# A decoder layer on one core: in each attention head the 896-column scan is ordered behind the third low part of the weights

## The chip, the cores and the metric

The kernel runs on one of the eight cores of a Trainium2 chip. A core has a matrix engine (TensorE, PE in the profile, its weight loads PEld), a vector engine (VectorE, DVE), a scalar engine for activations (ScalarE, ACT), a general engine (GpSimd, POOL) and a queue that issues transfers (SyncE, SP). Each engine takes its own instructions strictly in the order in which the built program lists them, and waits on semaphores for what others make. The metric is the device time of one execution in microseconds (us), as the median of several.

## The reference

One decoder layer over 1024 positions of width 1024, in float32: token mixing (stick-breaking attention, a state-space mixer, gates), cross-attention into 256 memory tokens, and a feed-forward block. The change lies in the stick-breaking attention, 16 heads of width 64:

```python
def stick_breaking_attention(q, k, v):
    ...
    for blk in range(seq // SB_BLOCK):          # 8 blocks of 128 queries
        t0 = blk * SB_BLOCK
        t1 = t0 + SB_BLOCK
        z = jnp.einsum('bhtd,bhsd->bhts', qf[:, :, t0:t1], kf[:, :, :t1])
        causal = jnp.arange(t1)[None, :] < (t0 + jnp.arange(SB_BLOCK))[:, None]
        log_1mb = jnp.where(causal, jax.nn.log_sigmoid(-z), 0.0)
        tail = lax.cumsum(log_1mb, axis=3, reverse=True)
        w = jnp.where(causal, jnp.exp(z + tail), 0.0)
        outs.append(jnp.einsum('bhts,bhsd->bhtd', w, vf[:, :, :t1]))
```

The weight of a key is its own sigmoid times the product of (1 - sigmoid) over all later keys. Written as differences of running products, that is one scan from the last key to the first.

## The kernel before

The layer is worked off in stages; the one that matters here is the attention stage (lines 770 to 1000 or so), from about 663 to 1086 us of the profiled execution. It handles the 16 heads one after the other, each in two halves of 512 queries, and each half in four blocks of 128 queries. Block b (0 to 7) sees L = (b + 1) x 128 keys.

`scores(h, half, tb, ...)` (lines 896 to 912) makes one block: products of queries and keys into PSUM (tile `sc`, lines 908 and 909), ACT's sigmoid of the negated scores into an SBUF tile `n` of L columns (line 910), and then one VectorE instruction over the L columns, from the last to the first (line 911): it multiplies the running value by the column's `n` and takes the maximum with a mask, so that it leaves running products with ones where the mask forbids the key. This text calls it the scan and names it by its width: 896 columns is block 6. Each tile name has one pool of four buffers for the first half of a head (`n` of up to 512 columns) and one for the second.

`values(h, half, ...)` (lines 915 to 952) turns the running products into outputs, in steps i over tiles of 128 keys. Step i transposes the key tile of the half's blocks on TensorE (tile `tr`, two PSUM buffers, line 925), and splits the result, minus one, into a high part on ACT (`wth`, line 928) and a low part on VectorE (`wtl`, line 929). Three steps later two products with the values, one with each part, add up in PSUM (`av`, lines 937 and 938). In the first half steps i = 0 to 3 make tiles of 512, 384, 256 and 128 columns, so the third low part (i = 2) is the one of 256 columns. In the second half there are four tiles of 512 and then 384, 256 and 128.

Beside these run the projections of the next pair of heads (`mm`, with weights split into `whi` and `wlo`, lines 115 to 132; queries, keys and their low parts `gt`, lines 849 to 870) and, once per pair of heads, a load of value differences and a subtraction on POOL (`va`, line 888) with their split (`v`, lines 115 and 122).

The order on each engine is not the order in which the functions are called. The calls are interleaved by shares (`interleave`), and a list scheduler then places every instruction by its own estimate of times. It pulls the scans of a head's second half ahead, so that they stand among the low parts of the half before. An instruction recorded under `behind([x])` may not be placed ahead of x. On one engine that adds no semaphore; it only fixes who goes first.

Of the kernel before, what the change touches and what calls it, by code (L numbers as in the profile page):

```python
# [8 lines left out]
F32 = mybir.dt.float32  # L9
# [3 lines left out]
ALU = mybir.AluOpType  # L13
# [3 lines left out]
P = 128  # L17
S = 1024
# [36 lines left out]
def hybrid_block(ctx, tc, a, out, dbg=None):  # L55
    nc = tc.nc
    V, A, T = [InTurn(tc, e) for e in (nc.vector, nc.scalar, nc.tensor)]
# [12 lines left out]
    def mk(pl, shape, dt, tag, bufs=None):  # L70
        uid[0] += 1
        kw = {} if bufs is None else {"bufs": bufs}
        return pl.tile(shape, dt, tag=tag, name=f"{tag}_{uid[0]}", **kw)
# [143 lines left out]
    def behind(marks):  # L217

        st = ExitStack()
        for m in marks:  # L220
            st.enter_context(tc.issue_after(m.ins))
        return st
# [52 lines left out]
    with ExitStack() as pa:  # L275
# [24 lines left out]
        with ExitStack() as p1:  # L300
# [135 lines left out]
            pt = mk(psp, [P, HALF], F32, "pdt", bufs=1)  # L436
# [4 lines left out]
            pt = mk(psp, [P, HALF], F32, "pv")  # L441
# [344 lines left out]
        with ExitStack() as p2:  # L786
# [13 lines left out]
            mask = mk(cb_, [P, S], BF16, "mask")  # L800
            V.memset(mask, 0.0)
            G.affine_select(mask[:, S - P:], mask[:, S - P:], [[-1, P]], ALU.is_gt, 1.0, base=0, channel_multiplier=1)

            marks, sig = [], []
            PIN = 8
            FQ = 1

# [73 lines left out]
            def differences(h):  # L881

                j = h % 2
                if j == 0:
                    va, vb = [mk(vp, [P, NCH, P], F32, n, bufs=1) for n in ("va", "vb")]
                    for t, r in ((va, 0), (vb, 1)):
                        nc.sync.dma_start(t, v_d[r:S + r, h * HD:(h + 2) * HD].rearrange("(c p) d -> p c d", p=P))
                    G.tensor_tensor(va, va, vb, ALU.subtract)
                    dvs[0] = va
                dv = dvs[0][:, :, j * HD:(j + 1) * HD]  # L890
                vt = mk(vp, [P, NCH, P], F32R, "v")
                hi_sb(vt[:, :, 0:HD], dv, "p")
                lo_of(vt[:, :, HD:P], dv, vt[:, :, 0:HD], G)
                heads[h]["v"] = vt

            def scores(h, half, tb, ns_):
                def run():
                    hd = heads[h]
                    if half == 0 and tb == 0:
                        differences(h)  # L900
                    b = half * 4 + tb
                    L = (b + 1) * P
                    nt = mk(bp, [P, (half + 1) * HALF], F32, f"n{half}")
                    ns_.append(nt)
                    for s0 in range(0, L, HALF):
                        s1 = min(L, s0 + HALF)
                        ps = mk(psc, [P, HALF], F32, "sc")[:, :s1 - s0]
                        T.matmul(ps, hd["qs"][:, b * P:(b + 1) * P], hd["kh"][:, s0:s1], start=True, stop=False)
                        marks.append(T.matmul(ps, hd["qs"][:, b * P:(b + 1) * P], hd["kl"][:, s0:s1], start=False, stop=True))
                        sig.append(A.activation(nt[:, s0:s1], ps, AF.Sigmoid, scale=-(HD ** -0.5)))  # L910
                    V.tensor_tensor_scan(nt[:, 0:L][:, ::-1], nt[:, 0:L][:, ::-1], mask[:, S - L:][:, ::-1], 1.0, ALU.mult, ALU.max)  # L911
                return run

            LAG = 3
# [1 line left out]
            def values(h, half, ns_):  # L916

                st = {}
                ni = 4 * (half + 1)

                def tr(i):
                    t0 = max(0, i - 4 * half)
                    pt = mk(pst, [P, HALF], F32, "tr")
                    for tb in range(t0, 4):
                        T.transpose(pt[:, tb * P:(tb + 1) * P], ns_[tb][:, i * P:(i + 1) * P], ident)  # L925
                    wh = mk(wt, [P, HALF], F32R, "wth")
                    wl = mk(wt, [P, HALF], F32R, "wtl")
                    A.activation(wh[:, t0 * P:], pt[:, t0 * P:], AF.Identity, bias=mone)  # L928
                    V.scalar_tensor_tensor(wl[:, t0 * P:], pt[:, t0 * P:], -1.0, wh[:, t0 * P:].bitcast(F32), ALU.add, ALU.subtract)  # L929
                    st[i] = (wh, wl, t0 * P)  # L930

                def av(i):
                    if i == 0:
                        st["po"] = mk(psv, [P, HALF], F32, "av")
                    po, vt = st["po"], heads[h]["v"]
                    wh, wl, off = st[i]
                    T.matmul(po[:, off:], vt[:, i, :], wh[:, off:], start=i == 0, stop=False)
                    marks.append(T.matmul(po[:, off:], vt[:, i, :], wl[:, off:], start=False, stop=i == ni - 1))  # L938
                    if i == ni - 1:
                        o = mk(t2, [P, HALF], F32, "oT")  # L940
                        A.activation(o, po, AF.Copy)
                        for j in range(2):
                            nc.sync.dma_start(o_d[j][h * HD:(h + 1) * HD, half * HALF:(half + 1) * HALF], o[j * HD:(j + 1) * HD])

                def step(i):
                    def run():
                        if i < ni:
                            tr(i)
                        if i >= LAG:
                            av(i - LAG)  # L950
                    return run

                return [step(i) for i in range(ni + LAG)]
# [25 lines left out]
            for m in range(NM):  # L979
                h, half = m // 2, m % 2  # L980
# [22 lines left out]
    with ExitStack() as p3:  # L1003
# [36 lines left out]
        marks = []  # L1040
# [409 lines left out]
    marks = []  # L1450
# [815 lines left out]
```

## Time and profile before

| | |
|---|---|
| median of 3 runs | 2505.12 us (2502.95 to 2508.58) |
| profiled execution | 2511.1 us |
| its span, first to last instruction | 2509.4 us |
| mean granted TensorE clock | 0.995 |
| PE busy (share of the span) | 2447.4 us (98%) |
| DVE busy | 1806.5 us (72%) |
| scans (L911), 128 of them | 190.0 us of DVE |
| low parts (L929), 192 of them | 99.7 us of DVE |

A row of the time order reads: start and length in us, engine, line, operation, out<-in by the program's names, partitions x elements, count (x2: two instructions in a row, shown as one), and in brackets the idle time of the engine just before it with what ended it. A row of the waits reads: who waited, for whom, us in total, times, the longest. A row of the stretches reads: the stretch, its length, and for PE, PEld, DVE, ACT and POOL the busy time with the number of instructions, then the granted clock, the DMA share and GB/s. Successive matmuls overlap: the length of one is longer than the distance to the next.

### The profile page before, as it was taken

How to read it: one execution, taken by the hardware profiler on the slowest of the kernel's cores; microseconds unless marked ns; L12 is line 12 of the kernel's file. 1: busy time of each engine (PE TensorE's matmuls, PEld its weight loads, DVE VectorE, ACT ScalarE, POOL GpSimd, SP SyncE). 2: the span in 40 equal slices, each digit the busy share in tenths (PEclk: the TensorE clock that was granted, in tenths of full speed). 3: DMA queues.
4: the chain of work that ended last, by engine and by line, in shares of the span. 5: the costliest groups of instructions: out<-in, count | busy, mean ns of one | idle time of the engine just before them, and what ended most of it. 6: DMA issues, size and time to landing. Idle time of an engine off the chain costs nothing. (4 is left out here: it accounts for less than half of the span.)

```text
span 2509.4 us, 33330 instructions
## 1 busy us (share of the span) xinstructions
PE 2447.4 (98%) x12306; PEld 2015.2 (80%) x12306; DVE 1806.5 (72%) x2237; ACT 1165.5 (46%) x2058; POOL 657.3 (26%) x545
## 2 busy tenths in 40 slices
PE   7999999999999999989999999999999999999998
PEld 5788888888778888877877778888888888888887
DVE  7665877776587888689898774487468655666997
ACT  5333455555465666466644312344435333344433
POOL 3221545443211111134444141102012332220001
PEclk9999999999999999999999999999999999999999
DMA  7431443333534343366332481331241322334322
GB/s 249 157 118 47 141 139 113 104 106 93 156 101 110 89 122 89 89 191 207 108 110 77 129 275 59 120 116 51 84 151 63 103 79 76 95 97 164 131 101 101
DMA packets 249132, 295.62 MB, mean 118 GB/s; under 512 B 17023, under 2 KB 169096, under 8 KB 248842
## 3 DMA queue, kind: packets, MB, share of 16 engines
q1 hardware_dynamic: 248682, 292.45, 37.0%
q8 instruction: 97, 1.59, 0.3%
q10 hardware_dynamic: 288, 1.05, 0.1%
q14 instruction: 65, 0.53, 0.1%
HBM read 202.20 MB, written 74.45 MB: 110 GB/s over the span
## 5 line engine op out<-in xcount | busy, mean ns | idle before, releaser
L911 DVE TENSOR_TENSOR_SCAN n<-n,mask 128x128 f32<-128x128 f32 (+7 forms) x128 | 190.0, 1511 | 24.5 <-ACT n L910 21.2
L122 DVE TENSOR_TENSOR sw<-sf,sw 128x512 fp32r<-128x512 f32 x142 | 126.9, 897 | 72.0 <-ACT sw L119 69.9
L119 ACT ACTIVATE sw<-sf 128x512 fp32r<-128x512 f32 x142 | 88.9, 628 | 155.8 <-PE mm L230 139.1
L928 ACT ACTIVATE wth<-tr,mone 128x512 fp32r<-128x512 f32 x192 | 110.7, 585 | 83.3 <-PE tr L925 81.3
L929 DVE SCALAR_TENSOR_TENSOR wtl<-tr,wth 128x512 fp32r<-128x512 f32 x192 | 99.7, 544 | 48.3 <-ACT wth L928 48.3
L693 DVE SCALAR_TENSOR_TENSOR b<-b,prmT,b 128x1023 f32<-128x1023 f32 (+2 forms) x72 | 109.6, 1522 | 16.9 <-ACT b L687 16.3
L122 DVE TENSOR_TENSOR sw<-wr,sw 128x512 fp32r<-128x512 f32 x107 | 99.2, 929 | 23.9 <-ACT sw L119 23.8
L196 POOL TENSOR_TENSOR sf<-wr,wr 128x512 f32<-128x512 f32 x36 | 53.2, 1477 | 229.8 <-DMA wr<-in_w_gu_dram 82.3
L229 PE MATMUL mm<-h,sw 128*128 128x512 f32 x288 | 112.0, 389 | 0.0
L230 PE MATMUL mm<-h,sw 128*128 128x512 f32 x288 | 111.7, 389 | 0.0
L910 ACT ACTIVATE n<-sc 128x512 f32<-128x512 f32 (+1 forms) x192 | 88.6, 494 | 46.6 <-PE tr L925 28.7
L228 PE MATMUL mm<-h,sw 128*128 128x512 f32 x288 | 109.9, 389 | 0.0
L125 PE MATMUL mm<-oth,bw 128*128 128x512 f32 x256 | 104.5, 408 | 3.9 <-DVE a L1259 2.3
L173 POOL TENSOR_SCALAR rstd<-ms 128x1 f32<-128x1 f32 x74 | 26.9, 363 | 307.8 <-ACT x L180 228.3
L127 PE MATMUL mm<-oth,bw 128*128 128x512 f32 x256 | 101.3, 396 | 0.0
L126 PE MATMUL mm<-otl,bw 128*128 128x512 f32 x256 | 101.1, 395 | 0.0
L127 PE MATMUL p<-bw,h 128*128 128x512 f32 x256 | 100.1, 392 | 0.5 <-DVE h L122 0.5
L126 PE MATMUL p<-bw,h 128*128 128x512 f32 x256 | 99.9, 390 | 0.0
L125 PE MATMUL p<-bw,h 128*128 128x512 f32 x256 | 99.7, 390 | 0.0
L925 PE MATMUL tr<-ident,n 128*128 128x128 f32 x576 | 95.4, 274 | 4.0 <-DVE wtl L929 4.0
L115 POOL TENSOR_SCALAR v<-va 128x512 fp32r<-128x512 f32 x16 | 20.6, 1289 | 286.8 <-PE av L938 165.9
L119 ACT ACTIVATE zh<-zr 128x512 fp32r<-128x512 f32 x72 | 45.0, 631 | 104.7 <-PE ma L492 52.3
(664 smaller groups left out, 7753.9 us busy)
## 6 DMA issues: line engine op xcount, KB each, us to landing
wr<-in_w_in_dram SPq DMA_DIRECT2D x36, 512.0 KB
wr<-in_w_gu_dram SPq DMA_DIRECT2D x72, 256.0 KB
zr<-in_w_in_dram SPq DMA_DIRECT2D x28, 512.0 KB
wraw<-in_w_in_dram SPq DMA_DIRECT2D x20, 512.0 KB
gu_d<-t SPq DMA_DIRECT2D x36, 256.0 KB
zs_d<-zo SPq DMA_DIRECT2D x32, 256.0 KB
xs_d<-b SPq DMA_DIRECT2D x32, 256.0 KB
kl<-gt SPq DMA_DIRECT2D x64, 128.0 KB
```

The lines of the kernel that those rows point to most:

```text
L119: A.activation(o, i, AF.Copy)
L122: eng.tensor_tensor(o, i, hi.bitcast(F32), ALU.subtract)
L125: first = T.matmul(ps, sh, mh, start=start, stop=False)
L126: T.matmul(ps, sh, ml, start=False, stop=False)
L127: T.matmul(ps, sl, mh, start=False, stop=stop)
L228: T.matmul(ps, w[0][:, k, :], bh, start=first and k == 0, stop=False, skip_group_check=True)
L229: T.matmul(ps, w[0][:, k, :], bl, start=False, stop=False, skip_group_check=True)
L230: ins = T.matmul(ps, w[1][:, k, :], bh, start=False, stop=last and k == 3, skip_group_check=True)
L693: V.scalar_tensor_tensor(acc[:, sh:], y[:, :S - sh], cw(3 - sh, f), acc[:, sh:], ALU.mult, ALU.add)
L911: V.tensor_tensor_scan(nt[:, 0:L][:, ::-1], nt[:, 0:L][:, ::-1], mask[:, S - L:][:, ::-1], 1.0, ALU.mult, ALU.max)
L928: A.activation(wh[:, t0 * P:], pt[:, t0 * P:], AF.Identity, bias=mone)
L929: V.scalar_tensor_tensor(wl[:, t0 * P:], pt[:, t0 * P:], -1.0, wh[:, t0 * P:].bitcast(F32), ALU.add, ALU.subtract)
```

## The change

The low parts are noted under head, half and step as they are made. The 896-column scan of a head (block 6, in its second half) is recorded behind the third low part of the same head's first half. The other seven scans of a head and everything else are recorded as before.

```diff
-            marks, sig = [], []
+            marks, sig, lows = [], [], {}
...
-                    V.tensor_tensor_scan(nt[:, 0:L][:, ::-1], nt[:, 0:L][:, ::-1], mask[:, S - L:][:, ::-1], 1.0, ALU.mult, ALU.max)
+                    with behind([lows[h, 0, 2]] if b == 6 else []):
+                        V.tensor_tensor_scan(nt[:, 0:L][:, ::-1], nt[:, 0:L][:, ::-1], mask[:, S - L:][:, ::-1], 1.0, ALU.mult, ALU.max)
...
-                    V.scalar_tensor_tensor(wl[:, t0 * P:], pt[:, t0 * P:], -1.0, wh[:, t0 * P:].bitcast(F32), ALU.add, ALU.subtract)
+                    lows[h, half, i] = V.scalar_tensor_tensor(wl[:, t0 * P:], pt[:, t0 * P:], -1.0, wh[:, t0 * P:].bitcast(F32), ALU.add, ALU.subtract)
```

What the scheduler makes of it shows in the order of the built programs. There a scan is listed as SCALAR_TENSOR_TENSOR with `mask` as its second input, the numbers in the names tell one tile from another, and lines behind 911 are one higher in the new kernel.

VectorE in head 3, around the end of head 2, before. The 896 scan (n_1137) stands between the 768 scan and the last two low parts of head 2 (wtl_6272, wtl_6286):

```order
L911 SCALAR_TENSOR_TENSOR n_1131_6358<-n_1131_6358,mask_5276 128x768
L911 SCALAR_TENSOR_TENSOR n_1137_6378<-n_1137_6378,mask_5276 128x896
L929 SCALAR_TENSOR_TENSOR wtl_6272<-tr_6268,wth_6271 128x256
L929 SCALAR_TENSOR_TENSOR wtl_6286<-tr_6283,wth_6285 128x128
L911 SCALAR_TENSOR_TENSOR n_1144_6403<-n_1144_6403,mask_5276 128x1024
L911 SCALAR_TENSOR_TENSOR n_1158_6465<-n_1158_6465,mask_5276 128x128
```

The same engine in head 3 now, from the key split of the next pair on. wtl_6334, 6355, 6375 and 6394 are the four low parts of head 3's first half, wtl_6448 the first of its second half:

```order
L863 TENSOR_TENSOR gt_6432<-mm_6324,kh_6304 128x512
L912 SCALAR_TENSOR_TENSOR n_1167_6493<-n_1167_6493,mask_5276 128x256
L912 SCALAR_TENSOR_TENSOR n_1176_6528<-n_1176_6528,mask_5276 128x384
L930 SCALAR_TENSOR_TENSOR wtl_6375<-tr_6371,wth_6374 128x256
L912 SCALAR_TENSOR_TENSOR n_1137_6378<-n_1137_6378,mask_5276 128x896
L930 SCALAR_TENSOR_TENSOR wtl_6394<-tr_6391,wth_6393 128x128
L912 SCALAR_TENSOR_TENSOR n_1184_6559<-n_1184_6559,mask_5276 128x512
L930 SCALAR_TENSOR_TENSOR wtl_6448<-tr_6442,wth_6447 128x512
```

The 896 scan went from ahead of head 2's last low parts to between the third and the fourth low part of head 3; the 256 scan of the next head (n_1167) moved down behind the key split too, where it had stood ahead of wtl_6355.

VectorE in head 4, in the same place as the piece above, before (the queries' split, then wtl_6651 and wtl_6670 as third and fourth low part, wtl_6726 the first of the second half):

```order
L854 TENSOR_TENSOR gt_6702<-mm_6600,qs_6586 128x512
L911 SCALAR_TENSOR_TENSOR n_1237_6763<-n_1237_6763,mask_5276 128x256
L911 SCALAR_TENSOR_TENSOR n_1246_6795<-n_1246_6795,mask_5276 128x384
L929 SCALAR_TENSOR_TENSOR wtl_6651<-tr_6647,wth_6650 128x256
L929 SCALAR_TENSOR_TENSOR wtl_6670<-tr_6667,wth_6669 128x128
L911 SCALAR_TENSOR_TENSOR n_1254_6826<-n_1254_6826,mask_5276 128x512
L929 SCALAR_TENSOR_TENSOR wtl_6726<-tr_6720,wth_6725 128x512
```

and now, with the head's 896 scan (n_1209), which had stood eleven rows further up:

```order
L854 TENSOR_TENSOR gt_6702<-mm_6600,qs_6586 128x512
L912 SCALAR_TENSOR_TENSOR n_1237_6763<-n_1237_6763,mask_5276 128x256
L912 SCALAR_TENSOR_TENSOR n_1246_6795<-n_1246_6795,mask_5276 128x384
L930 SCALAR_TENSOR_TENSOR wtl_6651<-tr_6647,wth_6650 128x256
L912 SCALAR_TENSOR_TENSOR n_1209_6657<-n_1209_6657,mask_5276 128x896
L930 SCALAR_TENSOR_TENSOR wtl_6670<-tr_6667,wth_6669 128x128
L912 SCALAR_TENSOR_TENSOR n_1254_6826<-n_1254_6826,mask_5276 128x512
L930 SCALAR_TENSOR_TENSOR wtl_6726<-tr_6720,wth_6725 128x512
```

All else in this piece kept its place: the scan was put in, and what stands behind it moved back by one.

TensorE in head 3, at the first step of its second half (tr_6442 takes the scanned tiles of blocks 4 to 7, of which n_1137 is block 6; av_6397 with wtl_6394 is the product of the first half's fourth low part; mm_6480 is a projection), before:

```order
L925 MATMUL tr_6442<-ident_88,n_1125_6337 128x128
L925 MATMUL tr_6442<-ident_88,n_1131_6358 128x128
L925 MATMUL tr_6442<-ident_88,n_1137_6378 128x128
L925 MATMUL tr_6442<-ident_88,n_1144_6403 128x128
L125 MATMUL mm_6480<-b11h_115,whi_6453 128x512
L126 MATMUL mm_6480<-b11l_116,whi_6453 128x512
L127 MATMUL mm_6480<-b11h_115,wlo_6454 128x512
L938 MATMUL av_6397<-wtl_6394,v_6184 128x128
```

and now:

```order
L926 MATMUL tr_6442<-ident_88,n_1125_6337 128x128
L926 MATMUL tr_6442<-ident_88,n_1131_6358 128x128
L125 MATMUL mm_6480<-b11h_115,whi_6453 128x512
L126 MATMUL mm_6480<-b11l_116,whi_6453 128x512
L127 MATMUL mm_6480<-b11h_115,wlo_6454 128x512
L926 MATMUL tr_6442<-ident_88,n_1137_6378 128x128
L926 MATMUL tr_6442<-ident_88,n_1144_6403 128x128
L939 MATMUL av_6397<-wtl_6394,v_6184 128x128
```

The transposes of blocks 6 and 7 moved behind three matmuls of the projection. In even heads the same is done with six.

TensorE in head 4, a little later, at the third step of the second half (tr_6754; n_1197, 1203, 1209 and 1216 are blocks 4 to 7; av_6781 with wth_6725 and wtl_6726 are the two products of the first step), before:

```order
L925 MATMUL tr_6754<-ident_88,n_1197_6613 128x128
L925 MATMUL tr_6754<-ident_88,n_1203_6634 128x128
L925 MATMUL tr_6754<-ident_88,n_1209_6657 128x128
L925 MATMUL tr_6754<-ident_88,n_1216_6682 128x128
L937 MATMUL av_6781<-wth_6725,v_6462 128x512
L938 MATMUL av_6781<-wtl_6726,v_6462 128x512
```

and now:

```order
L938 MATMUL av_6781<-wth_6725,v_6462 128x512
L926 MATMUL tr_6754<-ident_88,n_1197_6613 128x128
L926 MATMUL tr_6754<-ident_88,n_1203_6634 128x128
L926 MATMUL tr_6754<-ident_88,n_1209_6657 128x128
L926 MATMUL tr_6754<-ident_88,n_1216_6682 128x128
L939 MATMUL av_6781<-wtl_6726,v_6462 128x512
```

The product with the high part moved ahead of the third step's transposes; the one with the low part stayed behind them.

## The prediction

> **What bounds the kernel now.** I read the page's first part, then the stage of the change by stretches, then the waits of that stage, then the order of time in one head of each kind. The heads alternate: wherever I looked from head 1 to head 12, an odd head reads like head 3 and an even one like head 4, so these two stand for twelve.
>
> ```profile
> PE 2447.4 (98%) x12306; PEld 2015.2 (80%) x12306; DVE 1806.5 (72%) x2237; ACT 1165.5 (46%) x2058; POOL 657.3 (26%) x545
> 690.00:1002.00 312.00, 301.14 (x1636) 250.02 (x1635) 250.12 (x284) 189.44 (x381) 52.97 (x36) 1.00 0.40 103
> PE av L938 <- DVE wtl L929: 7.4, 6, 1.2
> PE tr L925 <- DVE wtl L929: 2.8, 6, 0.6
> PE sc L909 <- DMA kl<-gt: 0.7, 2, 0.5
> ```
>
> In the twelve heads (690 to 1002 us) TensorE idles 312.00 - 301.14 = 10.9 us at a granted clock of 1.00, and nearly all of it is three named waits: six of 1.2 us at a low-part product (odd heads), six of about 0.5 us at transposes (even heads), two on a DMA. TensorE is the bound; VectorE, at 250 of 312 us, decides when it waits. So the change, which gives no engine more or less work, is worth what it takes from and adds to TensorE's waits.
>
> **Odd heads: what is taken away.**
>
> ```profile
> 743.95 3.66 DVE L911 TENSOR_TENSOR_SCAN n<-n,mask 128x768 f32<-128x768 f32 x2
> 744.90 0.48 ACT L928 ACTIVATE wth<-tr,mone 128x256 fp32r<-128x256 f32 x1
> 746.09 1.08 ACT L910 ACTIVATE n<-sc 128x512 f32<-128x512 f32 x2
> 746.42 0.33 PE L937 MATMUL av<-wth,v 128*128 128x256 f32 x1
> 747.53 0.60 DVE L929 SCALAR_TENSOR_TENSOR wtl<-tr,wth 128x256 fp32r<-128x256 f32 x2
> 747.98 0.39 PE L938 MATMUL av<-wtl,v 128*128 128x256 f32 x1 [1.23 <-DVE wtl L929]
> L911 DVE TENSOR_TENSOR_SCAN n<-n,mask 128x896 f32<-128x896 f32 x13 | 26.2, 2012 | 0.7 <-ACT n L910 0.7
> ```
>
> The first row holds the 768 and the 896 scan. Behind them stands the low part that TensorE waits for, though its high part was ready at 745.38. Without the 896 scan (2.01 us, a net step of 1.92) that low part runs at 745.6 and ends at 746.0, and its product follows the product of 746.42 by 0.11, at 746.53 in place of 747.98: TensorE is 1.45 us early (the wait shown plus the emptied pipe).
>
> **Odd heads: what comes back.** The scan now stands between the third and fourth low part.
>
> ```profile
> 752.84 1.06 POOL L115 TENSOR_SCALAR whi<-wraw 128x1024 fp32r<-128x1024 f32 x1 [0.71 <-PE mm L126]
> 753.93 1.23 DVE L122 TENSOR_TENSOR wlo<-wraw,whi 128x1024 fp32r<-128x1024 f32 x1 [0.81 <-POOL whi L115]
> 755.67 0.95 DVE L911 TENSOR_TENSOR_SCAN n<-n,mask 128x384 f32<-128x384 f32 x1
> 756.54 0.59 DVE L929 SCALAR_TENSOR_TENSOR wtl<-tr,wth 128x256 fp32r<-128x256 f32 x2
> 757.06 1.23 DVE L911 TENSOR_TENSOR_SCAN n<-n,mask 128x512 f32<-128x512 f32 x1
> 757.41 0.28 PE L938 MATMUL av<-wtl,v 128*128 128x256 f32 x1
> 757.59 0.62 PE L925 MATMUL tr<-ident,n 128*128 128x128 f32 x4
> 758.74 0.22 PE L938 MATMUL av<-wtl,v 128*128 128x128 f32 x1
> 758.97 0.69 DVE L929 SCALAR_TENSOR_TENSOR wtl<-tr,wth 128x512 fp32r<-128x512 f32 x1 [0.68 <-ACT wth L928]
> ```
>
> From 753.93 to 758.3 VectorE has no gap, and the run's start hangs on POOL's whi, which hangs on TensorE. TensorE's 1.45 us, less what POOL's own queue lets through, bring that start forward by some 1.3 us, to 752.65. The 256 scan, which the new order puts there, takes 0.6 net. So the third low part ends at 756.26 (756.54 - 1.28 + 0.60 + 0.40), the 896 scan at 758.18, the fourth low part at 758.4. TensorE, 1.45 early, wants the third at 757.41 - 1.45 = 755.96 and waits 0.36. It then does two transposes and three matmuls (0.23 us apart), reaches the transpose of the 896 rows at 757.4 and waits 0.8. The product of 758.74 comes at 758.5. Of 1.45 us 0.25 are left. The first low part of the next half ends near 760.1 in place of 759.66; the transposes that wait for it stand at 762.3, so that costs nothing. The rest of the 2 us early VectorE has in between is lost in its wait for POOL. ACT's sigmoid for the 256 scan moves with it behind two copies and costs nothing (ACT is busy 189 of 312 us); on SP one load moves behind two stores at the end, beside other transfers. Six heads: -1.5 us. The DMA of kl follows a VectorE result that now comes 1.3 us sooner, so its 0.7 us go.
>
> Bounds for an odd head: nothing comes back, -1.45; the start at 753.93 does not move, and 1.28 us more come back, +1.0. I take -0.25, since POOL's row names a TensorE matmul as what it waits for.
>
> **Even heads.**
>
> ```profile
> 723.26 0.19 PEld L938 LDWEIGHTS av<-wtl,v 128*128 128x128 f32 x1 [0.21 <-DVE wtl L929]
> 779.06 1.23 DVE L122 TENSOR_TENSOR wlo<-wraw,whi 128x1024 fp32r<-128x1024 f32 x1 [0.54 <-ACT whi L119]
> 780.80 1.53 DVE L911 TENSOR_TENSOR_SCAN n<-n,mask 128x256 f32<-128x256 f32 x2
> 782.25 0.59 DVE L929 SCALAR_TENSOR_TENSOR wtl<-tr,wth 128x256 fp32r<-128x256 f32 x2
> 782.63 2.39 POOL L888 TENSOR_TENSOR va<-va,vb 128x1024 f32<-128x1024 f32 x1 [4.04 <-DMA va<-v_d]
> 782.77 3.33 DVE L911 TENSOR_TENSOR_SCAN n<-n,mask 128x512 f32<-128x512 f32 x1
> 783.70 0.62 PE L925 MATMUL tr<-ident,n 128*128 128x128 f32 x4
> 785.54 0.22 PE L938 MATMUL av<-wtl,v 128*128 128x128 f32 x1
> 786.02 0.66 DVE L929 SCALAR_TENSOR_TENSOR wtl<-tr,wth 128x512 fp32r<-128x512 f32 x1
> 786.74 0.66 PE L925 MATMUL tr<-ident,n 128*128 128x128 f32 x4 [0.53 <-DVE wtl L929]
> 787.47 0.39 PE L938 MATMUL av<-wtl,v 128*128 128x512 f32 x1
> ```
>
> Here the removal buys only the 0.2 us of the first row. The run from 779.06 starts when ACT's whi is there, which hangs on TensorE, so the 2 us saved earlier end in that wait. From 779.06 VectorE is booked through to the low part of 786.02, which TensorE already waits for. Into that run goes the 896 scan. The 512 scan costs 3.33 us here and 1.23 in the odd head: POOL's subtraction, 2.39 us, lies over it. Whichever scan meets the subtraction, these 2.1 us stay in the run. So the low part ends 2.01 us later, at 788.7, and the transposes of 786.74 move there. The new order has one product (0.32 us between 787.15 and 787.47, its place) ahead of them, which leaves 2.01 - 0.32 = 1.7, and 1.5 after the 0.2. Six heads: +9.0 us. Bounds: -0.2 if VectorE's run were not later at all, +1.8 if the moved product hides nothing.
>
> A rule bears on whether the subtraction's 2.1 us stay. The Trainium skill, "SBUF — State Buffer", section "Who interferes with whom", says that a VectorE instruction with two SBUF inputs and a GpSimd one that reads SBUF exclude each other, and that the first to start keeps the pair for the whole instruction. By it the subtraction, coming at 782.63 against about 782.57 for the moved scan, is let in between the two scans if not before, and 9.0 stands; were the port kept across neighbouring scans it would be nearly 0. The 3.33 against 1.23 agrees with the blocking; who wins between two scans no row above shows.
>
> **The ends.** Heads 0, 13, 14 and 15 have other surroundings.
>
> ```profile
> 1012.30 0.22 PE L938 MATMUL av<-wtl,v 128*128 128x128 f32 x1
> 1010.41 0.60 DVE L929 SCALAR_TENSOR_TENSOR wtl<-tr,wth 128x256 fp32r<-128x256 f32 x2
> 1075.33 1.28 DVE L929 SCALAR_TENSOR_TENSOR wtl<-tr,wth 128x512 fp32r<-128x512 f32 x2
> 1076.07 0.66 PE L925 MATMUL tr<-ident,n 128*128 128x128 f32 x4 [0.49 <-DVE wtl L929]
> ```
>
> Head 13 had no wait to lose: third low part to 1010.8, scan to 1012.7, fourth to 1012.9, so the product of 1012.30 comes 0.6 later. In head 15 the scan enters the run ahead of 1075.33, which TensorE waits for at 1076.07: 2.01 less a gap of half a microsecond, 1.5. Heads 0 and 14 I put at 0.5 each, like head 13. Together +3.1, between 0 and 6.
>
> **Sum.** -1.5 - 0.7 + 9.0 + 3.1 = +9.9 us. The profiled execution took 2511.1, 6.0 over the median; on the median of 2505.1 this gives 2515.0. Later stages give nothing back: their waits are for VectorE and ACT results that start from TensorE too. One rule speaks for slack. The Trainium skill, "Perfetto Trace Analysis", section "Identifying the Most-Contended Engine", holds matmul busy time to be a poor measure and takes LDWEIGHTS time instead; its 80% would leave a fifth of the span free, and the sum would be 0. The trace does not bear that out here: with loads busy 250 of 312 us TensorE has 10.9 us without a matmul.
>
> **Rivals.**
> Faster: the scan is free in its new place. One mechanism: the transposes of the 896 rows now stand three (odd) or six (even) matmuls later, 0.7 or 1.4 us, and if the scan's 2.01 us end by then in every head, and the low part behind does not matter, all waits named vanish but those at transposes: -8.7 - 0.7 - 1.2 + 3.1 = -7.5, 2497.6. It decides for faster once an even head costs under about -0.6 with the odd heads as I have them, or under 0.2 if they keep 1.45. Against it: 786.74 already waits.
> Cancelled: the scans go back to back ahead of the subtraction, which then lies over low parts that read PSUM. The even head's run is 782.57 + 2.01 + 0.28 + 1.23 = 786.1, as now. Sum -1.5 - 0.7 - 1.2 + 3.1 = -0.3: 2504.8. For it: 782.57 against 782.63; against it, only one scan of two need meet the subtraction.
> Dearer: POOL's whi does not come earlier in odd heads; six times 1.28 us more, +17.6, 2522.7.
>
> **Chances.** As forecast (2509 to 2521) 0.65, dearer 0.12, cancelled 0.15, faster 0.08. A measurement of this kernel tells no change from one under 0.2%, 5 us: slower is the first two less 0.03 of the forecast's low edge, 0.74; same 0.15 + 0.03 = 0.18; faster 0.08. The range leaves out the faster case, the lower part of the cancelled one and little at the top: 2503 to 2523. The forecast's own is 2509 to 2521.
>
> **What would show it.** In odd heads the wait of the low-part product (7.4 us, 6 times) gone, and a new wait of transposes or the fourth low-part product behind the 896 scan, about 1.1 us a head with the third's. In even heads VectorE's run without a gap up to the first 512-wide low part, and TensorE's wait there near 2.2 us in place of 0.5, or split with one at the moved transposes. TensorE's idle time in the twelve heads about 20 us in place of 10.9 (the sum's +6.8 there, and some 0.2 us an old wait of emptied pipe that is no idle time now). Wrong it would be if VectorE's run in even heads began earlier than TensorE dictates, or if a 512 scan there took 1.2 us.

## The result, and the profile after

| | before | after |
|---|---|---|
| median of 20 runs | 2508.06 us (2502.95 to 2510.43) | 2512.98 us (2508.25 to 2516.08) |
| profiled execution, and its span | 2511.1, 2509.4 us | 2510.95, 2509.2 us |
| idle time of TensorE, 690 to 1002 us | 10.9 us | 13.9 us |

The changed kernel is slower: ratio 1.0022, 95% interval 1.0016 to 1.0028, which is 4.0 to 7.0 us. A second comparison on another occasion gave 1.0023 (1.0014 to 1.0032). With 20 runs the kernel before stands 3 us higher than with the three that the prediction started from. One execution of the later experiments (odd heads, earlier place) took 11176 us, and no ratio counts it.

The page of the changed kernel, first part; then the twelve heads as one stretch, and TensorE's waits in it:

```profile
PE 2442.5 (97%) x12306; PEld 2010.9 (80%) x12306; DVE 1804.8 (72%) x2237; ACT 1160.7 (46%) x2058; POOL 674.7 (27%) x545
690.00:1002.00 312.00, 298.13 (x1616) 247.27 (x1615) 244.97 (x281) 184.41 (x376) 67.84 (x36) 0.99 0.40 103
PE tr L926 <- DVE wtl L930: 6.1, 6, 1.0
PE av L938 <- ACT oT L942: 4.4, 6, 0.7
PE tr L926 <- DVE n L912: 3.3, 6, 0.6
```

The six waits of 1.2 us for a low part are gone, and so are the waits for kl. In their place stand six of 0.55 us behind the moved scan (odd heads), six of 1.0 us at transposes and six of 0.74 us at a product that waits for ACT's copy of outputs (even heads).

The profiled executions differ by nothing although the medians differ by 4.9 us. The two traces tell why: the granted clock (the share of its full speed that TensorE is allowed) drops for some microseconds at places that only partly repeat from one execution to the next. First row before, second row after; then the changed kernel just ahead of such a drop (a dip, below) and in it:

```profile
1460.00:1500.00 40.00, 39.00 (x159) 31.27 (x160) 34.61 (x29) 7.44 (x7) 26.89 (x17) 0.91 0.89 304
1460.00:1500.00 40.00, 37.70 (x164) 30.11 (x163) 33.79 (x29) 8.07 (x8) 27.07 (x17) 1.00 0.95 322
936.11:939.52 3.41, 1.68 (x10) 0.99 (x8) 3.41 (x3) 1.75 (x3) 1.72 (x1) 1.00 0.23 69
939.52:942.93 3.41, 3.38 (x11) 2.79 (x12) 1.26 (x2) 0.69 (x1) 0.00 (x0) 0.50 0.66 203
```

A clock of 0.91 over 40 us costs 3.6 us. The kernel before lost that at 1460 us and the changed one did not; the changed one had a dip at 939.5 us (last row: 3.41 us at 0.50, about 1.7 us of clock). Over the whole span the mean granted clock is 0.995 before and 0.997 after. So I compare the two traces matmul by matmul within the attention stage. At its end the changed kernel is 4.7 us later than at its start, some 1.5 of it from that dip. That leaves 3.2 us for the order, against 4.9 (4.0 to 7.0) by the medians.

**An odd head.** Head 3 of the changed kernel in order of time:

```profile
746.85 0.33 PE L938 MATMUL av<-wth,v 128*128 128x256 f32 x1
747.02 0.28 PE L939 MATMUL av<-wtl,v 128*128 128x256 f32 x1
748.78 1.54 POOL L115 TENSOR_SCALAR v<-va 128x512 fp32r<-128x512 f32 x1 [13.87 <-PE av L939]
752.74 1.22 DVE L122 TENSOR_TENSOR wlo<-wraw,whi 128x1024 fp32r<-128x1024 f32 x1 [1.11 <-POOL whi L115]
755.94 0.40 DVE L930 SCALAR_TENSOR_TENSOR wtl<-tr,wth 128x256 fp32r<-128x256 f32 x1
756.25 2.01 DVE L912 TENSOR_TENSOR_SCAN n<-n,mask 128x896 f32<-128x896 f32 x1
756.39 0.39 PE L939 MATMUL av<-wtl,v 128*128 128x256 f32 x1
758.32 0.44 PE L926 MATMUL tr<-ident,n 128*128 128x128 f32 x2 [0.55 <-DVE n L912]
758.51 0.31 PE L939 MATMUL av<-wtl,v 128*128 128x128 f32 x1
```

Read against the rows of the prediction: the product before the old wait is 0.43 us later than in the trace before (746.42, now 746.85), the one that waited 0.96 earlier (747.98, now 747.02). A little behind it all stand 1.02 earlier, which makes 1.45 us saved. The third low part's product is still 1.02 earlier (757.41, now 756.39) and does not wait. The transposes of the 896 rows wait 0.55 us, and behind them the matmuls are 0.10 earlier. The head has gained 0.53 us. At the products with kl, whose transfer they waited for before, another 0.74 comes.

**An even head.** Head 4:

```profile
777.97 1.23 DVE L122 TENSOR_TENSOR wlo<-wraw,whi 128x1024 fp32r<-128x1024 f32 x1 [0.30 <-ACT whi L119]
781.48 2.02 DVE L912 TENSOR_TENSOR_SCAN n<-n,mask 128x896 f32<-128x896 f32 x1
781.80 3.85 POOL L888 TENSOR_TENSOR va<-va,vb 128x1024 f32<-128x1024 f32 x1 [4.07 <-DMA va<-v_d]
783.41 0.26 DVE L930 SCALAR_TENSOR_TENSOR wtl<-tr,wth 128x128 fp32r<-128x128 f32 x1
783.59 3.14 DVE L912 TENSOR_TENSOR_SCAN n<-n,mask 128x512 f32<-128x512 f32 x1
785.21 0.59 ACT L942 ACTIVATE oT<-av 128x512 f32<-128x512 f32 x1
785.85 0.50 PE L938 MATMUL av<-wth,v 128*128 128x512 f32 x1 [0.74 <-ACT oT L942]
786.66 1.25 DVE L930 SCALAR_TENSOR_TENSOR wtl<-tr,wth 128x512 fp32r<-128x512 f32 x2
787.37 0.66 PE L926 MATMUL tr<-ident,n 128*128 128x128 f32 x4 [1.02 <-DVE wtl L930]
787.78 0.48 PE L939 MATMUL av<-wtl,v 128*128 128x512 f32 x1
```

VectorE's run starts 1.09 earlier than before (779.06, now 777.97), and its first 512-wide low part comes 0.64 later (786.02, now 786.66): the run is 1.73 us longer. TensorE now waits twice. The product that the new order put ahead of the transposes opens a new sum in `av`, of which there is one buffer, so it needs ACT's copy of the half before (785.21, done at 785.80). ACT's copy stands behind the high part of the first tile, and that one behind the transposes that moved behind six matmuls. Then the transposes wait for the low part as before, only longer. At 787.78 the head is 0.31 late, and it settles at 0.18: from -0.84 at its beginning, +1.02 us. The other even heads give +1.0 to +1.2.

### The profile page after: what moved, and what is told of

It is laid out like the page before. It is cut to its first block, busy times and chain, and to the rows that moved or that the text cites. A ratio compares the mean times of both kernels' runs of the same rounds, so it can differ in the third digit from the quotient of the medians.

```text
span 2509.2 us, 33318 instructions
## 1 busy us (share of the span) xinstructions
PE 2442.5 (97%) x12306; PEld 2010.9 (80%) x12306; DVE 1804.8 (72%) x2237; ACT 1160.7 (46%) x2058; POOL 674.7 (27%) x545
## 5 line engine op out<-in xcount | busy, mean ns | idle before, releaser
L115 POOL TENSOR_SCALAR v<-va 128x512 fp32r<-128x512 f32 x16 | 28.2, 1764 | 278.8 <-PE av L939 278.7
L926 PEld LDWEIGHTS tr<-ident,n 128*128 128x128 f32 x576 | 69.4, 141 | 32.9 <-DVE wtl L930 12.5
```

## The experiments

Each was timed in five rounds beside the kernel before. The idle time is that of TensorE in 690 to 1002 us of the profiled execution (312 less the busy time of the stretch).

| | median, us | ratio to before, 95% interval | TensorE idle, us |
|---|---|---|---|
| odd heads alone | 2502.45 | 0.9975 (0.9965 to 0.9985) | 5.7 |
| even heads alone | 2516.21 | 1.0036 (1.0024 to 1.0049) | 18.4 |
| odd heads, earlier place | 2506.65 | 0.9999 (0.9990 to 1.0008) | 7.7 |
| change, and 512 scan later | 2501.55 | 0.9982 (0.9973 to 0.9992) | 7.8 |
| odd heads alone, and 512 scan later | 2500.43 | 0.9971 (0.9960 to 0.9982) | 3.3 |
| 512 scan later, no tie | 2501.40 | 0.9980 (0.9971 to 0.9990) | 8.5 |
| before, no subtraction | 2517.09 | 1.0036 (1.0023 to 1.0049) | 7.8 |
| change, no subtraction | 2515.18 | 1.0037 (1.0024 to 1.0049) | 8.1 |
| odd + 512 later, piece on ACT | 2499.36 | 0.9970 (0.9959 to 0.9980) | 3.8 |
| odd earlier, piece on ACT | 2502.00 | 0.9981 (0.9973 to 0.9990) | 3.2 |
| odd earlier + 512 later, piece on ACT | 2499.40 | 0.9967 (0.9955 to 0.9979) | 1.3 |
| the change again | 2512.74 | 1.0023 (1.0014 to 1.0032) | 13.9 |

### Where the loss sits: odd heads alone, even heads alone

```diff
-with behind([lows[h, 0, 2]] if b == 6 else []):
+with behind([lows[h, 0, 2]] if b == 6 and h % 2 == 1 else []):    # the second kernel: == 0
```

> The tie only in odd heads, the rest as before. Theory of the booked run: the terms of the odd and the even heads add up and don't touch one another. In the changed kernel's trace an odd head is 0.55 us ahead of before, the transfer of kl in heads 3, 7 and 11 another 1.4 together, heads 13 and 15 lose 0.3 and 0.4: 6 x -0.55 - 1.4 + 0.7 = -4.0 us against before, so faster by some 0.16%, with TensorE's wait of 1.2 us for the low part gone and one of 0.55 us at transposes behind the scan in its place. Rival, the loss is not in the even heads (any new order of the matmuls or the clock costs it): no faster than before, -1 to +3 us.

> The tie only in even heads. Theory of the booked run: each even head costs 1.1 us (VectorE's run ahead of the first 512-wide low part is longer by the scan), head 0 another 0.4: 6 x 1.1 + 0.4 = +7 us, slower than the whole change, the 1.2 us waits in odd heads and the kl waits still there. Rival, the loss is not in the even heads: about half of what the whole change costs, +2.5 us or less.

TensorE's waits in the twelve heads, odd heads alone and then even heads alone:

```profile
PE tr L926 <- DVE n L912: 3.3, 6, 0.6
PE tr L926 <- DVE wtl L930: 2.4, 6, 0.5
```

```profile
PE av L939 <- DVE wtl L930: 7.2, 6, 1.2
PE tr L926 <- DVE wtl L930: 6.1, 6, 1.0
PE av L938 <- ACT oT L942: 4.4, 6, 0.7
```

The waits split without remainder: each half of the change brings its own and leaves the other's nearly as they were. Odd heads alone are 0.25% faster (expected 4.0 us, measured 6.3, interval 3.8 to 8.8; 3.9 by the medians, and 4.3 to 4.9 in the stage of its trace, by where its start is taken). Even heads alone are 0.36% slower (expected 7; interval 6 to 12; 6.9 in the stage). The loss is in the even heads, and the odd heads hide part of it.

### The even heads: VectorE's run, and what lies under it

First the scan that closes the run is put behind the low part that TensorE waits for, with the change and without any tie:

```diff
-with behind([lows[h, 0, 2]] if b == 6 else []):
+with behind([lows[h, 0, 2]] if b == 6 else [lows[h - 1, 1, 0]] if b == 3 and h % 2 == 1 else []):    # the second kernel: only the part for b == 3
```

> The change, and beside it the next head's 512 scan (block 3 of odd heads), which closes VectorE's run in even heads, is put behind the first 512-wide low part. Theory of the booked run: that low part waits then only for ACT's high part (785.3 us in head 4 of the changed kernel's trace, in place of 786.66), TensorE's wait of 1.0 us at the transposes goes, the 0.74 us at the moved product may stay: 6 x -1.0 = -6 us against the change, about -1 us against before. Rival, the even heads' cost is not the run on VectorE but the moved product, which waits for ACT to have copied the head's earlier outputs: the 512 scan changes nothing or little, +3 to +5 us against before.

> Only the 512 scan of odd heads behind the first 512-wide low part of the head before; no 896 scan is tied. Theory: the six waits of 0.5 us at transposes in even heads go, the 1.2 us waits in odd heads stay: -3 us. Rival, handed on to the second low part: 0.

Waits with the change, then without any tie:

```profile
PE av L938 <- ACT oT L942: 4.5, 6, 0.7
PE tr L926 <- DVE n L912: 3.3, 6, 0.6
```

```profile
PE av L939 <- DVE wtl L930: 7.2, 6, 1.2
```

With one scan out of the run the six waits of 1.0 us are gone, and the six of 0.74 us stay, as the theory of the booked run had it. Against before the change stands at 1.0022 and this kernel at 0.9982, 10 us apart, where I expected 6; its stage of the trace is 4.1 us faster than before, which makes 7 against the change's 3.2. The change's drops of the clock (below), of which this trace has none in the twelve heads, can be part of the rest. Without a tie this edit alone removes the 0.5 us waits of the even heads. That is 0.2% (expected 3 us, interval 2.5 to 7.3).

Then POOL's subtraction was left out, in both kernels. They use the loaded values in place of the differences and so compute something else; only their times count here:

```diff
-                    G.tensor_tensor(va, va, vb, ALU.subtract)
```

> The kernel before without POOL's subtraction of the values (the value differences are left out: the loaded values themselves are used). Theory of the port: the 512 scan in even heads takes 1.2 us in place of 3.3, VectorE's run ends 2.1 us sooner, TensorE's 0.5 us waits there go: -3 us. Rival, the scan is 3.3 us long for another reason: no change.

> The changed kernel without POOL's subtraction (left out as in the run beside it). Theory: without those 2 us the moved scan fits into VectorE's run: the 1.0 us wait at the transposes goes, the wait of the moved product for ACT's copy stays, an even head costs 0.2 us in place of 1.1; odd heads as before: 6 x (-0.55 + 0.2) - 1.4 + 1.1 = -2.4 us against before without the subtraction, so about -5 us against before. Rival, the tie costs its 2 us in even heads with or without the subtraction: +3 to +5 us against before without it, 0 to +2 against before.

Before without it: the 512 scan of an even head, its waits in the twelve heads, and a wait at the start of the stage. Then the same of the change without it, with the scan of the same head:

```profile
791.04 1.21 DVE L910 TENSOR_TENSOR_SCAN n<-n,mask 128x512 f32<-128x512 f32 x1
PE av L937 <- DVE wtl L928: 7.2, 6, 1.2
PE sc L907 <- DMA kh<-kh: 6.7, 1, 6.7
```

```profile
790.31 1.21 DVE L911 TENSOR_TENSOR_SCAN n<-n,mask 128x512 f32<-128x512 f32 x1
PE av L937 <- ACT oT L941: 4.4, 6, 0.7
PE tr L925 <- DVE n L911: 3.3, 6, 0.6
PE sc L907 <- DMA kh<-kh: 6.9, 1, 6.9
```

Both kernels are slower than before because TensorE waits almost 7 us for a transfer of kh at the start of the stage. I did not follow that up; they are to be compared with each other. The 512 scan takes 1.21 us, not 3.3 or 3.1, so the 2 us are the subtraction's. Without it no wait at the even heads' transposes is left, before and after. The tie then adds 0.3 us of idle time to the twelve heads (7.8 to 8.1), where with the subtraction it adds 3.0. But my number of -2.4 us between the two was wrong. It was made of -3.5 in the twelve heads and +1.1 at the ends, and the two traces, taken matmul by matmul, give -1.7 in the twelve heads. The times can't tell: the medians differ by -1.9 with ranges that overlap, the ratios to before (1.0036 and 1.0037) not at all, so what follows rests on the traces. An even head still costs 0.5 us, because the moved product waits for ACT's copy, and I had set that at 0.2. So of the 1.1 us that an even head costs, about 0.6 are VectorE's run with the subtraction in it, and about 0.5 lie under it as a second wait that decides as soon as the first is gone.

### The odd heads: what hands the gain back

```diff
+with behind([lows[h - 1, 1, 7]] if b == 6 and h % 2 == 1 else []):
```

> In odd heads the 896 scan goes only behind the last low part of the head before, two rows later than before the change; even heads as before. Theory: what odd heads give back in the change (0.55 us at the transposes of the 896 rows, 0.9 with the emptied pipe) is due to the far place between the third and fourth low part; here the 1.45 us are kept for the most part: 6 x -1.2 - 1.4 = -8.6 us, range -6 to -10. Rival: the scan delays the 1024 scan and the low parts behind it as it did before, TensorE, now earlier, meets them there, and the wait is only handed on: -1 to -4 us.

The expectation was wrong, and the rival too in its reason. Waits, POOL and VectorE in head 3 of this kernel, with a wait behind the stage as last row:

```profile
PE av L939 <- DVE wtl L930: 4.7, 6, 0.8
744.66 4.88 DVE L912 TENSOR_TENSOR_SCAN n<-n,mask 128x896 f32<-128x896 f32 x3
746.58 2.70 POOL L115 TENSOR_SCALAR v<-va 128x512 fp32r<-128x512 f32 x1 [14.29 <-PE av L939]
751.71 1.23 DVE L122 TENSOR_TENSOR wlo<-wraw,whi 128x1024 fp32r<-128x1024 f32 x1 [1.11 <-POOL whi L115]
PE pst L125 <- ACT s2r L119: 1.9, 1, 1.9
```

and the same piece of POOL's in the kernel before:

```profile
750.04 0.70 POOL L115 TENSOR_SCALAR v<-va 128x512 fp32r<-128x512 f32 x1 [15.98 <-PE tr L925]
```

The 1.2 us wait is gone, and 0.8 us come back at the third low part. POOL's split of the value differences, which takes 0.70 us by itself, came just as the 896 scan ended and the 1024 scan began. It took 2.70 us, and POOL's weight split behind it, on which VectorE's run hangs, was late with it (by some 0.8 us against the next kernel's, at 750.62 and 747.80, with that trace 2.0 us ahead there). In the stage the trace shows 3.1 us gained. By the medians nothing is left: the schedule of the following stage came out otherwise (the last row is a wait that the kernel before does not have there), and this stretch also had dips of the clock. How the two share the loss stays open.

To try that reading, the piece was given to ACT, here and in the kernel with odd heads alone and the later 512 scan:

```diff
-                hi_sb(vt[:, :, 0:HD], dv, "p")
+                hi_sb(vt[:, :, 0:HD], dv, "a" if j == 0 else "p")
```

> As odd_early, with the same piece made by ACT. Theory: in odd_early the scans of 896, 1024 and 128 columns follow each other without a gap and hold POOL's piece up to 2.70 us; that is what made VectorE's run, and with it the third low part, late by the 0.8 us that TensorE waits there. Without it the split comes about 0.7 us sooner: the wait of 0.8 us shrinks to 0.1 to 0.2, 6 x -0.65 = -4 us against odd_early. Rival, the three scans themselves make the low parts late: the 0.8 us stay, no change against odd_early.

> The tie in odd heads alone, and the 512 scan that closes VectorE's run in even heads (block 3 of the next, odd head) behind the first 512-wide low part. Theory: the two gains add: odd_only's -4.9 us in its trace's attention stage, and TensorE's wait of 0.5 us at the transposes in heads 2 to 12, also in 14: -4.9 - 6 x 0.5 = -8 us against before. Rival: the scan then delays the second 512-wide low part and the wait is only handed on: no better than odd_only, -4 to -6.

> As odd_512late, and the high part of the next even head's value differences is made by ACT in place of POOL (in the trace of odd_512late POOL needs 1.54 us for it while VectorE's 1024 scan runs, and 0.70 where it meets none). Theory: in odd heads VectorE's run starts when POOL's weight split is there, and that stands behind this piece; without it the split comes 0.5 us sooner, and TensorE's wait of 0.55 us at the transposes of the 896 rows all but goes: 6 x -0.5 = -3 us against odd_512late, -10 against before. Rival: the start hangs on TensorE alone, or ACT's own queue is late by the 0.6 us that it gets: no change or slower than odd_512late, -7 or more.

In the earlier place, with the piece on ACT, one wait and the same places of POOL and VectorE:

```profile
PE av L939 <- DVE wtl L930: 0.7, 4, 0.2
745.54 2.29 POOL L122 TENSOR_TENSOR v<-va,v 128x512 fp32r<-128x512 f32 x1 [15.37 <-ACT v L119]
749.08 1.21 DVE L122 TENSOR_TENSOR wlo<-wraw,whi 128x1024 fp32r<-128x1024 f32 x1
```

The 0.8 us waits shrink to 0.2, and the time falls by 4.7 us against the run without this edit, taken on another occasion (4.5 by the two ratios; expected 4). The rival is out: the three scans in a row are not shorter here (5.57 us in place of 4.88, since POOL's next piece, at 2.29 us in place of 1.29, now holds the last of them), and the low part comes in time all the same. In the change's place, first without and then with the piece on ACT:

```profile
749.31 1.04 POOL L115 TENSOR_SCALAR whi<-wraw 128x1024 fp32r<-128x1024 f32 x1
PE tr L926 <- DVE n L912: 3.3, 6, 0.6
```

```profile
746.96 1.06 POOL L115 TENSOR_SCALAR whi<-wraw 128x1024 fp32r<-128x1024 f32 x1 [0.28 <-PE mm L126]
PE tr L926 <- DVE n L912: 3.8, 7, 0.6
```

Here the rival was right: the weight split no longer waits behind POOL's own piece but 0.28 us for a matmul, and the 0.55 us stay. VectorE's run begins no sooner (0.06 us once the 2.3 us by which this trace is ahead are taken off). So in an odd head two chains reach the weight split at nearly the same time, TensorE's and POOL's; in the change's place TensorE's decides, in the earlier place POOL's. The kernel without the edit, odd heads alone and the later 512 scan, is 0.29% faster than before (expected 8 us, interval 4.5 to 10). By TensorE's idle time the two gains add: 5.2 and 2.4 us less each alone, 7.6 together. The times (0.25% and 0.20% alone) leave it open, since their intervals are as wide as the smaller gain.

### All that paid, and the change once more

> What has paid so far, together: in odd heads the 896 scan right behind the last low part of the head before, with ACT making the high part of the value differences (odd_early_vact, -5.3 us by its medians), and the 512 scan behind the first 512-wide low part in even heads (3 to 5 us by itself). Theory: the terms add, as they did in odd_512late: -8 to -10 us against before, 2498. Rival: they hinder each other (in odd heads the run starts earlier, in even heads ACT and the second low part are later), no better than odd_512late, -7.

> The changed kernel once more on the chip of the run beside it, for a second trace of the attention stage: by the theory the same waits to 0.1 us in the twelve heads (6 x 0.55 at transposes in odd heads, 6 x 0.74 at the moved product and 6 x 1.0 at transposes in even heads), and a dip of the granted clock at 940 us only if it belongs to the change, not if it comes by chance. Time +4 to +6 us against before.

The earlier place, the later 512 scan and the piece on ACT together:

```profile
PE av L939 <- DVE wtl L930: 1.0, 6, 0.2
690.00:1002.00 312.00, 310.72 (x1685) 257.21 (x1683) 247.76 (x295) 197.24 (x397) 58.16 (x32) 1.00 0.41 105
```

TensorE is idle 1.3 us of 312. At 2499.4 us the kernel beats both the one before (0.9967) and the changed one, but by the intervals not the simpler kernel with two ties (0.9971). So the forecast of 8 to 10 us and its rival, 7, are not told apart (8.3, interval 5.3 to 11.3).

The change once more showed the same three waits with the same sums (6.1, 4.4 and 3.3 us), and three dips of the clock in the twelve heads, at other places than the first trace's one. One of them, the stretch ahead of it first:

```profile
785.31:788.72 3.41, 1.71 (x11) 1.02 (x9) 3.41 (x3) 1.75 (x3) 1.75 (x1) 1.00 0.26 77
788.72:792.13 3.41, 3.35 (x11) 2.77 (x12) 1.29 (x3) 0.69 (x1) 0.00 (x0) 0.50 0.71 211
```

All four dips of the two traces of the change look like this: TensorE idled 1.71 to 1.76 us in the 3.41 us ahead, and that is an even head's two waits, 0.74 and 1.02 us, falling into one such stretch. None of the other twelve traces has a dip in these heads; of them only even heads alone has the pair of waits, and there no stretch between two possible starts of a dip held more than 1.63 us of idle time. So the dips come with the change's pair of waits, 1.7 us each, and come or not by how the pair falls. That can be why the medians show more than the order's 3.2 us; how many an execution has on average no run shows.

## Why the prediction was right, and where its sum was off

The forecast was slower, 2515.0 us, with a range of 2503 to 2523; measured were 2512.98. The range also holds the kernel before (2508.06), so a time inside it says little by itself; that the change is slower, and which heads make it so, came as forecast. The change itself was forecast at +9.9 us and came to +4.9. That the time lies closer than the change is luck: the base taken, 2505.1, was 3 us below the median of more runs. Term by term, in the two profiled executions:

| step | forecast, us | measured, us |
|---|---|---|
| six odd heads | -1.5 | -3.3 (-0.53 to -0.57 each) |
| transfer of kl | -0.7 | -1.4 (heads 3, 7, 11: 0.74, 0.54, 0.16) |
| six even heads | +9.0 | +6.8 (1.0 to 1.2 each) |
| heads 0, 13, 14, 15 | +3.1 | +1.1 (0.4, 0.3, 0, 0.4) |
| sum | +9.9 | +3.2 |

- **Odd heads, what is taken away:** right to the hundredth, 1.45 us.
- **Odd heads, what comes back:** the mechanism was right, the transposes of the 896 rows waiting for the scan. The size was off. VectorE's run was to start 1.3 us sooner, and started 1.62 sooner (753.93 to 752.74, with the head itself 0.43 later), so that the third low part made no wait in place of 0.36, and the transposes 0.55 in place of 0.8 (the sign named was about 1.1 us a head). The bound with a start that does not move, and the rival "dearer" built on it, fell.
- **Even heads:** the booked run is what costs most there, and "even heads alone" shows the place. The term was mis-sized: the run grew by 1.73 us, not 2.01 (the scan shifts the next one by 1.91, and the 512 scan, 3.14 in place of 3.33, meets less of the subtraction). The moved product hid the 0.32 us that it was to hide and the earlier start gave its 0.2, and 0.1 to 0.2 us more were made up behind the wait, where successive matmuls follow each other closely again: 1.0 to 1.2 in place of 1.5. What the forecast did not see is that the moved product, counted only as work that hides 0.32 us, has a wait of its own for ACT's copy. It costs nothing extra here, since the low part comes later still, but it is the floor under any repair.
- **POOL's subtraction:** as forecast it was let in between the two scans and the 2 us stayed in the run, so "cancelled" did not happen. The rows show it: the scan that began at 781.48 was not slowed (2.02 us), the subtraction that began at 781.80 took 3.85, and the scan behind it 3.14. Between the two scans stands a low part (783.41), which takes one of its inputs from PSUM; so head 4 does not show who wins between two scans without a gap. The Trainium skill, "SBUF — State Buffer", section "Who interferes with whom", calls the port pair that the two engines share an exclusive lock, and says of VectorE's two-port modes that whoever issues first has it for the whole instruction. The trace agrees for a scan with two SBUF inputs, with those three numbers.
- **The ends:** too dear by 2 us. They were put at the price of heads read only in part.
- **The signs named in advance:** the 1.2 us waits are gone (yes); a wait in even heads near 2.2 us (1.76, split in two); idle time about 20 us (13.9).
- **The clock:** the sum held nothing for it. The dips behind the even heads' pair of waits, 1.7 us each, come on top of the +3.2.
- **A bound among the rivals:** with the odd heads and ends as forecast (-1.5 - 0.7 + 3.1 = +0.9), an even head had to cost under -1.0, not -0.6, for the change to gain the 5 us that can be told apart.
- **"Faster: the scan is free in its new place":** no; but what it named holds for odd heads alone, which are faster.

## What to carry to other kernels

Where heads or tiles alternate, price a reordering for each kind and try it on each kind alone: here one edit was a gain of 5 us in one half of the heads and a loss of 7 in the other. What counts for a moved instruction is whether the run that it joins has a gap before the next result that the bound engine waits for; here taking a scan out of that run gained 0.2% by itself, as much as the tie cost. And a matmul that is moved forward brings its own waits along, above all the one for its accumulator, which nothing shows as long as it stands late. Two short waits close together can also cost a third time, through the clock.

## What the runs showed of the hardware

- A POOL instruction that reads SBUF was held off by VectorE's two-input scans until they ended, one that has a single input too: the same 128x512 split took 0.70, 1.54 and 2.70 us by what was running on VectorE.
- Between two scans that follow each other at once, POOL got in if it was already waiting: with odd heads in the earlier place and the piece on ACT, POOL's piece began to wait at 745.54 us, during the 1024 scan, and the 128 scan behind it took 1.46 us (0.42 in the heads with no POOL work beside it). When the piece came in the same moment as the second scan (odd heads, earlier place: 746.58 us), the scan went first, and the piece took 2.70 us.
- The granted TensorE clock of this program on one core dropped to 0.50 for 3.41 or 6.83 us, a few times per execution. Between 70 and 2400 us the 14 traces have 57 such drops. The starts within one trace are whole multiples of 3.41 us apart, and each comes right behind a stretch of 3.41 us in which TensorE was idle for 1.5 to 3.3 us. On the same grid, stretches with over 1.8 us idle were always followed by a drop, those between 1.5 and 1.8 some of the time, those under 1.5 never. That idle time is the cause is not tested by a run of its own.
- The two drops weighed in the first traces cost about 1.7 and 3.6 us, as much as the effects measured, so single traces can be compared only stage by stage.
